# Decoder block on one core: attention scores on all 128 rows, and the gate projections moved beside and behind attention

## Chip, core and metric

The kernel runs on one core of a Trainium2 chip. The metric is device microseconds of one execution; lower is better. Engines are named as the profile names them: PE (TensorE, matmuls), PEld (its weight loads), DVE (VectorE), ACT (ScalarE), POOL (GpSimd), SP (SyncE, which issues most DMAs). L480 is line 480 of the kernel before.

## What is computed

One decoder block for a sequence of 512 tokens and 1024 channels, in float32. Cut to what matters here:

```python
mod = silu(c) @ w_ada + b_ada;  sh1, sc1, g1, sh2, sc2, g2 = split(mod, 6)
proj = (rms_norm(x, pre_norm1) * (1 + sc1) + sh1) @ w_in      # 1024 x 7168
u_glu, q, k, v, gate_logits = proj split into 2048, 1024, 1024, 1024, 2048
u = conv31(ua * sigmoid(ub));  y_conv = silu(layer_norm(u)) @ conv_w_out + conv_b_out
att = softmax(q1 k1^T) v - lam * softmax(q2 k2^T) v           # causal, 8 heads, rope on q and k
y = (g_conv * y_conv + g_att * head_norm(att)) @ w_o          # gates: sigmoid(gate_logits)
x = x + g1 * rms_norm(y, post_norm1)
h = rms_norm(x, pre_norm2) * (1 + sc2) + sh2
x = x + g2 * rms_norm(square(relu(h @ w_ff1)) @ w_ff2, post_norm2)
```

## The kernel before, in words

**Products.** Each float32 operand is split into a high part, rounded to float32r, and a low part, the exact rest; a product is three float32r matmuls, high·high, high·low, low·high (mm3, L205). A projection tile is 128 columns of w_in for all 512 tokens: 8 steps of k with three matmuls of 512 columns (proj, L284). Weights come by SP in loads of 512 KB into three raw buffers; ACT makes the high part, and DVE or ACT with an adding DMA the low part (sub_w, L156).

**Stages on PE.** The start; five pairs of convolution inputs (glu, L537 to L541); 16 gate tiles in a row, evacuated by ACT with a Sigmoid (L543 to L549); four groups of two heads, each with tiles q1, k1, q2, k2 (rope_a, rope_b) and the v tiles (L738 to L749); 8 tiles of the convolution's output (yc, L785); the product with w_o (y, L871 to L883), each of whose four 128-token blocks needs the row gate G1 before its two PSUM banks come free (residual, L819; two such blocks fit into PSUM, L872); then the MLP.

**Attention.** A group's heads are worked in 8 units, each of one head and 128 queries (heads, L611). A unit's scores need, for each of the two softmaxes, three matmuls: L626 multiplies [q high; q low] (128 rows) by [k high; k high]; L627 multiplies q's high 64 rows by k's low 64 rows; L628 adds the causal mask as a bf16 identity times a bf16 mask. ACT does Exp, DVE the maximum, the factors and the difference; PE transposes it (turn) and multiplies by v (weigh). rope_b builds the stacked tiles with four SP DMAs of 128 KB for each q and each k. k's low part stays where DVE wrote it (k_lo). The last DVE steps of a head are norm (L684), scale_out (L693) and turn_back (L702).

**What sets the order of the work beside.** Python generators emit the work beside the projections, and a clock says when. A k-step of a projection ticks 0.65, one of v 0.33 (tick, L252). A tick adds dt times a rate to the background account; each whole unit emits one step of the first generator in the background list, which holds, in this order, conv_steps (124 steps of two DVE multiply-adds), conv_norm (17 steps, L425) and modulations (30 steps, L498). An attention group's generator is resumed when the clock has passed the pause that it named (d1, d2, d3). Program order is the priority with which the compiler's list scheduler fills each engine's queue; on the chip each queue then runs in order. DVE steps of the background are also pinned behind the ninth last DVE operation of the foreground (Beside, L226; lag 8): they can't be placed much ahead of where they were emitted. Before the yc tiles a loop (L753) emits at once what is left of conv_steps and conv_norm. What is left of the modulations is emitted before the eighth yc tile (end_attention, L779).

**Modulations** make s2, sh2 and g1, in that order, by halves of 512 columns: 24 loads of 512 KB (raw_a, L480) into a single buffer, each followed by two DVE operations (L483, L485; under line L235 in the profile), and after four loads a PE transpose and a DVE sum (modc, L492). gate_rows (L510) makes the rows G1 from g1 with eight DVE diagonals, matmuls and ACT copies. The rates before are 0.7 beside u, 0.65 beside the gates, 0.7 beside the first group, 0.5 beside the others, 0.4 beside yc.

Of the kernel before, what the change touches and what calls it, by code (L numbers as in the profile page):

```python
# [17 lines left out]
P = 128  # L18
# [6 lines left out]
CW = 31  # L25
PAD = CW - 1
DFF = 4 * D
EPS = 1e-6
LAM_INIT = 0.2
NEG = -1e30  # L30

CFG = {'raw': 3, 'hi': 3, 'lo': 3, 'ahead': 1, 'araw': 1, 'qk': 10, 'vb': 3, 'plane': 5, 'dma_u': 3, 'dma_g': 1, 'dma_r': 3, 'dma_c': 0, 'dma_o': 0, 'dma_f1': 0, 'dma_f2': 0, 'dma_first': 1, 'r_u': 0.7, 'r_g': 0.65, 'r_p0': 0.7, 'r_p': 0.5, 'r_c': 0.4, 'd1': 2, 'd2': 0.6, 'd3': 0.6, 'evac': 200, 'mod_pe': ((0, 0), (0, 1)), 'wa': 6, 'f_dve': 1, 'wn': 1, 'tail': 2, 'co_att': 7, 'nsplit': 2, 'lag': 8, 'rope_dma': 1, 'ada_dma': 0, 'r_a': 0.15, 'rb': 1, 'tail0': 0, 'sc_dve': 1, 'deep': 1, 'alb': 2, 'h2_act': 0, 'fpre': 2, 'mod_wait': 1, 'pin_mod': 0, 'pin_aT': 0, 'pin_oT': 0, 'ada_rl': 0, 'av_copy': 1, 'nfore': 2, 'kfore': 4, 'wo_at': 5}

# [10 lines left out]
def block_kernel(ctx, tc, io, out):  # L44
# [29 lines left out]

# [1 line left out]
    p0_stack = ExitStack()  # L76
# [28 lines left out]

    ones = const.tile([P, P], F32, name="ones")
    nc.vector.memset(ones, 1.0)
    onesd = const.tile([P, P], F32, name="onesd")
# [4 lines left out]
    nc.vector.memset(epsc, EPS)  # L113
    identb = const.tile([P, P], BF16, name="identb")
    maskb = const.tile([P, P], BF16, name="maskb")

# [11 lines left out]
    def group(slot, name, width=T):  # L128
        w = PAD + T if slot == "U" else T
        pairs = [None] * (KT // 2)  # L130

        def at(ct, sl=slice(0, width)):
            i = ct // 2
            if pairs[i] is None:
                pairs[i] = planes.tile([P, 2, w], F32, tag=f"{slot}{i}", name=f"{name}{i}")
            return pairs[i][:, ct % 2, sl]

        def pair(i):
            at(2 * i)
            return pairs[i]  # L140

        at.pair = pair
        return at
# [10 lines left out]
    nsplit = {}  # L154

    def sub_w(hi, lo, raw, kind):  # L156
        """hi = raw rounded to float32r, lo = the exact rest."""
        nc.scalar.copy(r32(hi), raw)  # L158
        n = nsplit[kind] = nsplit.get(kind, 0) + 1
        every = CFG.get("dma_" + kind, 0)  # L160
        if kind == "first" and n <= CFG["f_dve"]:
            every = 0
        if every == 1 or (every > 1 and n % every):
            nc.scalar.activation(r32(lo), raw, AF.Copy, scale=-1.0)
            nc.gpsimd.dma_start(r32(lo), raw, accum_op=ALU.add)
        else:
            vec.tensor_tensor(r32(lo), raw, hi, ALU.subtract)
# [25 lines left out]

    # weight tiles in the order of their use, split a few tiles ahead of it
    w_specs, w_ready = [], []
# [13 lines left out]

# [39 lines left out]
    clk = dict(t=0.0, bg=0.0, ada=0.0, rate=0.0, resume=0.0)  # L249
# [41 lines left out]
    for ct in range(nfirst, KT):  # L291
        w_specs += [(w_cols, w_in, ct * P, "ua", "u"), (w_cols, w_in, D + ct * P, "ub", "u")]
    for ct in range(KT):
        w_specs += [(w_cols, w_in, 5 * D + ct * P, "gate", "g"), (w_cols, w_in, 6 * D + ct * P, "gate", "g")]
    for g in range(NH // 2):
        for c0 in (2 * D, 3 * D, 2 * D + T, 3 * D + T):
            w_specs.append((w_cols, w_in, c0 + g * P, "qk", "r"))
        w_specs += [(w_v, g, 0), (w_v, g, 1)]
    for ct in range(KT):
        w_specs.append((w_cols, w_co, ct * P, "co", "c"))  # L300

# [1 line left out]
    cwr = p0.tile([CW, D], F32, name="cwr")  # L303
# [25 lines left out]
    for k0, nk in (((0, 1), (1, 1), (2, 2), (4, 2), (6, 2)) if CFG["wn"] == 2 else [(k, 1) for k in range(KT)]):  # L329
# [13 lines left out]
        for j in range(nk):  # L343
# [3 lines left out]
            for i in range(2):  # L347
# [3 lines left out]
                else:  # L351
                    nc.tensor.matmul(po[:, i:i + 1], accs[i][:, js], ones[:, 0:1], start=True, stop=True)
            nc.vector.scalar_tensor_tensor(s1[:, k:k + 1], po[:, 0:1], bada1[:, 8 + k:9 + k], pre1[:, k:k + 1], ALU.add, ALU.mult)
# [21 lines left out]
    make_causal_mask(nc, maskf, NEG)  # L375
    nc.vector.tensor_copy(maskb, maskf)
    nc.vector.tensor_copy(identb, ident)
    pt = ps_t("pb_t")
# [26 lines left out]

# [1 line left out]
    u_done = [False] * KT  # L407
# [102 lines left out]
    def gate_rows(cols, slot):  # L510
        """the columns as rows, the same on every partition"""
        rows = post.tile([P, 2, T], F32, tag=slot, name=f"rows_{slot}")
        for half in range(2):
            dg = plane("diag")
            for i in range(4):
                ct = half * 4 + i
                vec.tensor_scalar(dg[:, i * P:(i + 1) * P], ident, cols[:, ct:ct + 1], None, ALU.mult)
            po = ps_t("rows")
            nc.tensor.matmul(po, ones, dg, start=True, stop=True)
            nc.scalar.copy(rows[:, half], po)  # L520
# [21 lines left out]

    clk["rate"] = CFG["r_g"]  # L543
    for ct in range(KT):
        for dst in (GC, GA):
            o = ps_proj("gate")
            proj(HH, HL, o)
            with tc.high_priority(offset=CFG["evac"]):
                nc.scalar.activation(dst(ct), o, AF.Sigmoid)  # L549

# [1 line left out]
    def rope_a(is_q, name):  # L552
        """projection, and the rotated halves on their way"""
        o = ps_proj(name)
# [10 lines left out]

    def rope_b(part, after):
        is_q, name, f, _ = part
# [4 lines left out]
        A, B = slice(0, HD), slice(HD, P)  # L572
        if is_q:
            hi, lo = plane("qhi"), plane("qlo")
        else:
            hi, lo = plane("khi"), qk("lo")
        with tc.issue_after(after) if CFG["rb"] else ExitStack():
            nc.scalar.copy(r32(hi), f)
        vec.tensor_tensor(r32(lo), f, hi, ALU.subtract)
        t0, t1 = qk("t0"), qk("t1")  # L580
        other = lo if is_q else hi
        nc.sync.dma_start(t0[A], hi[A])
        nc.sync.dma_start(t0[B], other[A])
        nc.sync.dma_start(t1[A], other[B])
        nc.sync.dma_start(t1[B], hi[B])
        return t0, t1, lo

# [23 lines left out]
    def heads(g, q, kk, vts):  # L611
# [3 lines left out]
        def scores(j, qb):  # L615
            rows = slice(j * HD, (j + 1) * HD)
            n = (qb + 1) * P
# [5 lines left out]
            for b in range(2):  # L623
                qt, kt, klo = q[b][j], kk[b][j], kk[b][2]
                o = s[:, b, 0:n]
                nc.tensor.matmul(o, r32(qt[:, qs]), r32(kt[:, 0:n]), start=True, stop=False)  # L626
                nc.tensor.matmul(o, r32(qt[rows, qs]), r32(klo[rows, 0:n]), start=False, stop=False)  # L627
                nc.tensor.matmul(s[:, b, qs], identb, maskb, start=False, stop=True)  # L628
            nm = small("nm", 2)
# [108 lines left out]
    for g in range(NH // 2):  # L738
        clk["rate"] = CFG["r_p"] if g else CFG["r_p0"]
        qk, part = [], None  # L740
        for is_q, name in ((True, "q1"), (False, "k1"), (True, "q2"), (False, "k2")):
            nxt = rope_a(is_q, name)
            if part:
                qk.append(rope_b(part, ins_of(nxt[3])))
            part = nxt
        vts, k2 = v_tiles(g, lambda after: rope_b(part, after))
        q1, k1, q2 = qk
        drain_att()
        att_q.append(heads(g, (q1, q2), (k1, k2), vts))  # L749

# [1 line left out]
    left = 0 if CFG["ada_dma"] else 1  # L752
# [64 lines left out]

# [1 line left out]
    def residual(tb, hv, gr):  # L819
# [64 lines left out]

# [1 line left out]
    F0, F1 = group("HH", "f0"), group("HL", "f1")  # L886
# [113 lines left out]
```

## Time and profile before

| what | value |
|---|---|
| time, median of 3 runs (lowest to highest) | 948.25 us (947.97 to 951.44) |
| span of the profiled execution | 947.9 us |
| busy PE / DVE / ACT / POOL | 884.9 / 585.6 / 420.2 / 118.8 us |
| PE stages: gates / groups / yc / y (stretches read from the trace) | 133 to 220 / 220 to 446 / 446 to 517 / 517 to 578 us |
| mean granted TensorE clock | 0.978 of full speed |

The span is the profiled execution's own time, from the first to the last instruction. A busy share is an average over stages with different limits. Matmuls overlap in the records, so what one costs is read from the distance between two starts.

### The profile page before, as it was taken

How to read it: one execution, taken by the hardware profiler on the slowest of the kernel's cores; microseconds unless marked ns; L12 is line 12 of the kernel's file. 1: busy time of each engine (PE TensorE's matmuls, PEld its weight loads, DVE VectorE, ACT ScalarE, POOL GpSimd, SP SyncE). 2: the span in 40 equal slices, each digit the busy share in tenths (PEclk: the TensorE clock that was granted, in tenths of full speed). 3: DMA queues.
4: the chain of work that ended last, by engine and by line, in shares of the span. 5: the costliest groups of instructions: out<-in, count | busy, mean ns of one | idle time of the engine just before them, and what ended most of it. 6: DMA issues, size and time to landing. Idle time of an engine off the chain costs nothing. (4 is left out here: it accounts for less than half of the span.)

```text
span 947.9 us, 11572 instructions
## 1 busy us (share of the span) xinstructions
PE 884.9 (93%) x4147; PEld 714.6 (75%) x4147; DVE 585.6 (62%) x1084; ACT 420.2 (44%) x770; POOL 118.8 (13%) x162
## 2 busy tenths in 40 slices
PE   6878999999889999798899889999999999999996
PEld 5666888888768777667677668878888788888885
DVE  4857999995679887678699865343222323443522
ACT  4554444544355668644253354433433444223310
POOL 2111011113415142213000011000000000000000
PEclk9999999999989999799899999999999999999999
DMA  9987588988958584875645830464333322232411
GB/s 298 291 212 183 145 178 186 203 189 191 220 111 193 130 175 93 189 191 143 188 155 157 268 88 1 121 179 144 89 89 95 105 89 90 96 105 89 156 44 45
DMA packets 141194, 140.13 MB, mean 148 GB/s; under 512 B 6842, under 2 KB 113459, under 8 KB 141138
## 3 DMA queue, kind: packets, MB, share of 16 engines
q1 hardware_dynamic: 131362, 111.98, 39.7%
q0 software_dynamic: 9696, 27.40, 17.1%
q8 instruction: 32, 0.52, 0.2%
q14 instruction: 24, 0.20, 0.1%
q10 hardware_dynamic: 80, 0.03, 0.0%
HBM read 101.51 MB, written 2.10 MB: 109 GB/s over the span
## 5 line engine op out<-in xcount | busy, mean ns | idle before, releaser
L220 DVE TENSOR_TENSOR lo_ff<-raw_ff,hi_ff 128x1024 fp32r<-128x1024 f32 x56 | 68.5, 1225 | 121.4 <-ACT hi_ff L158 121.4
L158 ACT CAST hi_ff<-raw_ff 128x1024 fp32r<-128x1024 f32 x56 | 58.9, 1052 | 183.0 <-PE ff L207 102.0
L235 DVE SCALAR_TENSOR_TENSOR acc<-u,cw,acc 128x512 f32<-128x512 f32 x200 | 135.3, 738 | 0.0
L206 PE MATMUL ff<-h2h,hi_ff 128*128 128x512 f32 (+2 forms) x272 | 105.3, 388 | 0.0
L207 PE MATMUL ff<-h2l,hi_ff 128*128 128x512 f32 (+2 forms) x272 | 104.3, 384 | 0.0
L208 PE MATMUL ff<-h2h,lo_ff 128*128 128x512 f32 (+2 forms) x272 | 104.2, 384 | 0.0
L208 PE MATMUL f<-hi_ff,fl 128*128 128x512 f32 x192 | 74.7, 389 | 0.0
L207 PE MATMUL f<-lo_ff,fh 128*128 128x512 f32 x192 | 74.7, 389 | 0.0
L206 PE MATMUL f<-hi_ff,fh 128*128 128x512 f32 x192 | 74.7, 389 | 0.0
L563 POOL DMA_DIRECT2D qf<-qs x64 | 52.2, 1284 | 102.1 <-DVE f L220 39.6
L206 PEld LDWEIGHTS ff<-h2h,hi_ff 128*128 128x128 f32 x272 | 51.0, 188 | 11.2 <-issue 0.5
L208 PEld LDWEIGHTS ff<-h2h,lo_ff 128*128 128x128 f32 x272 | 51.2, 188 | 11.0 <-issue 0.2
L207 PEld LDWEIGHTS ff<-h2l,hi_ff 128*128 128x128 f32 x272 | 51.4, 189 | 10.4 <-issue 0.2
L220 DVE TENSOR_TENSOR fl<-f,fh 128x512 fp32r<-128x512 f32 x32 | 22.1, 691 | 59.9 <-PE f L207 55.4
L150 POOL TENSOR_SCALAR ss<-ss 128x1 f32<-128x1 f32 x12 | 3.7, 307 | 403.2 <-ACT junk L824 393.8
L235 DVE SCALAR_TENSOR_TENSOR ada<-raw_a,cs,ada 128x512 f32<-128x512 f32 x56 | 41.9, 748 | 16.2 <-DMA raw_a<-in_w_ada_dram 15.8
L206 PE MATMUL gate<-hh,hi_gate 128*128 128x512 f32 x128 | 49.8, 389 | 0.0
L207 PE MATMUL gate<-hl,hi_gate 128*128 128x512 f32 x128 | 49.8, 389 | 0.0
L208 PE MATMUL gate<-hh,lo_gate 128*128 128x512 f32 x128 | 49.8, 389 | 0.0
L633 ACT ACTIVATE p<-s,nm 128x128 f32<-128x128 f32 (+3 forms) x64 | 33.3, 525 | 29.8 <-DVE nm L220 21.4
L207 PEld LDWEIGHTS f<-lo_ff,fh 128*128 128x128 f32 x192 | 36.0, 188 | 7.6
L206 PEld LDWEIGHTS f<-hi_ff,fh 128*128 128x128 f32 x192 | 36.0, 188 | 7.6
(252 smaller groups left out, 2148.7 us busy)
## 6 DMA issues: line engine op xcount, KB each, us to landing
raw_ff<-in_w_ff_dram SPq DMA_DIRECT2D x56, 512.0 KB
raw_a<-in_w_ada_dram SPq DMA_DIRECT2D x32, 512.0 KB
wa<-in_w_ada_dram SPq DMA_DIRECT2D x16, 512.0 KB
raw_gate<-in_w_in_dram SPq DMA_DIRECT2D x16, 512.0 KB
lo_gate<-raw_gate POOLq DMA_DIRECT2D x16, 512.0 KB, 5.9
raw_qk<-in_w_in_dram SPq DMA_DIRECT2D x16, 512.0 KB
lo_qk<-raw_qk POOLq DMA_DIRECT2D x12, 512.0 KB, 5.8
raw_v<-in_w_in_dram SPq DMA_DIRECT2D x8, 512.0 KB
```

Source lines behind the costliest of these rows:

```text
L150: nc.gpsimd.tensor_scalar(ms[:, 0:1], ms[:, 0:1], ms[:, 1:2] if ms.shape[1] == 2 else 0.0, EPS, ALU.add, ALU.add)
L158: nc.scalar.copy(r32(hi), raw)
L206: nc.tensor.matmul(o, r32(sh), r32(mh), start=first, stop=False)
L207: nc.tensor.matmul(o, r32(sh), r32(ml), start=False, stop=False)
L208: plog[:] = [nc.tensor.matmul(o, r32(sl), r32(mh), start=False, stop=last)]
L220: ins = op(*args, **kw)
L235: return op(*args, **kw)
L563: nc.gpsimd.dma_start(f[b * 32:(b + 1) * 32], sw[s:s + 32], accum_op=ALU.add)
L633: nc.scalar.activation(p[b][:, 0:n], s[:, b, 0:n], AF.Exp, bias=nm[:, b:b + 1], accum_out=lsm[:, b * NTB + qb:b * NTB + qb + 1])
```

## The change

1. Scores: k's low part gets a stacked tile of its own, [k low; k low], so that L627 uses all 128 rows of q's stacked tile. Four more SP DMAs for each k (eight in place of four). The pairs of low tiles live in the buffers of the conv gates (GC), alternating between groups. Low parts of k are first written to the general plane buffers.
2. The mask matmul is float32r times float32r in place of bf16.
3. Gates: the attention gates of heads 2g and 2g+1 are projected right after group g's v tiles; the eight conv gates come after the last group, in the order 4 to 7, 0 to 3, so that a buffer is free when its gate is written.
4. Rates and pauses: 0.45 beside groups and gates; the pauses are 2.6, 1.0, 1.0 in place of 2, 0.6, 0.6.
5. Small: U's rows are padded from 542 to 544 elements; the 128x128 tile of ones becomes one column, and gate_rows uses the tile of 1/1024 with its diagonals scaled by 1024.

```diff
-CFG = {... 'r_g': 0.65, 'r_p0': 0.7, 'r_p': 0.5, ... 'd1': 2, 'd2': 0.6, 'd3': 0.6, ...}
+CFG = {... 'r_g': 0.45, 'r_p': 0.45, ... 'd1': 2.6, 'd2': 1.0, 'd3': 1.0, ...}
-        w = PAD + T if slot == "U" else T
+        w = UW if slot == "U" else T
-    identb = const.tile([P, P], BF16, name="identb")
-    maskb = const.tile([P, P], BF16, name="maskb")
+    identr = const.tile([P, P], F32, name="identr")
+    maskr = const.tile([P, P], F32, name="maskr")
-    for ct in range(KT):
-        w_specs += [(w_cols, w_in, 5 * D + ct * P, "gate", "g"), (w_cols, w_in, 6 * D + ct * P, "gate", "g")]
...
         w_specs += [(w_v, g, 0), (w_v, g, 1)]
+        w_specs += [(w_cols, w_in, 6 * D + ct * P, "gate", "g") for ct in (2 * g, 2 * g + 1)]
+    conv_gates = (4, 5, 6, 7, 0, 1, 2, 3)
+    for ct in conv_gates:
+        w_specs.append((w_cols, w_in, 5 * D + ct * P, "gate", "g"))
...
-                vec.tensor_scalar(dg[:, i * P:(i + 1) * P], ident, cols[:, ct:ct + 1], None, ALU.mult)
+                vec.tensor_scalar(dg[:, i * P:(i + 1) * P], ident, cols[:, ct:ct + 1], float(D), ALU.mult, ALU.mult)
-            nc.tensor.matmul(po, ones, dg, start=True, stop=True)
+            nc.tensor.matmul(po, onesd, dg, start=True, stop=True)
...
-    clk["rate"] = CFG["r_g"]
-    for ct in range(KT):
-        for dst in (GC, GA):
-            o = ps_proj("gate")
-            ...
+    def gate(dst, ct):
+        o = ps_proj("gate")
+        proj(HH, HL, o)
+        with tc.high_priority(offset=CFG["evac"]):
+            nc.scalar.activation(dst(ct), o, AF.Sigmoid)
...
-            hi, lo = plane("qhi"), plane("qlo")
-        else:
-            hi, lo = plane("khi"), qk("lo")
+        hi, lo = plane(f"{name}hi"), plane(f"{name}lo")
...
+        i = 2 * (1 - g % 2) + int(name[1]) - 1
+        kl = planes.tile([P, 2, T], F32, tag=f"GC{i}", name=f"kl{i}")
+        for j, (t, half) in enumerate(((t0, A), (t1, B))):
+            for rows in (A, B):
+                nc.sync.dma_start(t[rows], hi[half])
+                nc.sync.dma_start(kl[rows, j], lo[half])
+        return t0, t1, kl
...
-                nc.tensor.matmul(o, r32(qt[rows, qs]), r32(klo[rows, 0:n]), start=False, stop=False)
-                nc.tensor.matmul(s[:, b, qs], identb, maskb, start=False, stop=True)
+                nc.tensor.matmul(o, r32(qt[:, qs]), r32(kl[:, j, 0:n]), start=False, stop=False)
+                nc.tensor.matmul(s[:, b, qs], r32(identr), r32(maskr), start=False, stop=True)
...
         att_q.append(heads(g, (q1, q2), (k1, k2), vts))
+        for ct in (2 * g, 2 * g + 1):
+            gate(GA, ct)
+    clk["rate"] = CFG["r_g"]
+    for ct in conv_gates:
+        gate(GC, ct)
```

## Rows read from the trace of the kernel before

**Rows 1.** Busy time, share of the span and instructions, by engine (the page).

```profile
PE 884.9 (93%) x4147; PEld 714.6 (75%) x4147; DVE 585.6 (62%) x1084; ACT 420.2 (44%) x770; POOL 118.8 (13%) x162
```

**Rows 2.** Busy time by stretch: gates, groups, yc, y.

```profile
core 0: us, PE busy (x) PEld busy (x) DVE busy (x) ACT busy (x) POOL busy (x), PEclk, DMA share, GB/s
133.00:220.00 87.00, 87.00 (x385) 72.09 (x384) 82.93 (x126) 40.71 (x49) 13.91 (x16) 1.00 0.91 192
220.00:446.00 226.00, 205.10 (x1117) 164.69 (x1115) 172.32 (x356) 130.75 (x303) 67.30 (x80) 0.95 0.71 162
446.00:517.00 71.00, 66.25 (x308) 50.31 (x308) 57.92 (x117) 28.90 (x79) 6.00 (x6) 0.95 0.58 167
517.00:578.00 61.00, 54.07 (x250) 41.15 (x250) 44.02 (x86) 27.91 (x67) 6.58 (x13) 1.00 0.50 153
```

**Rows 3.** PE's waits: engine, line, releaser: us in total, times, longest.

```profile
PE s L626 <- DMA k_t<-khi: 6.1, 1, 6.1
```

**Rows 4.** PE in order of time: y's third block starts (in brackets idle before, releaser).

```profile
550.15 0.50 PE L206 MATMUL y<-woh,yh 128*128 128x512 f32 x1 [1.26 <-DVE t L220]
```

**Rows 5.** DVE in order of time: start, duration; modulations begin, g1 ends.

```profile
382.77 0.68 DVE L235 TENSOR_TENSOR z<-acc,rl 128x512 f32<-128x512 f32 x1
383.37 0.48 DVE L235 TENSOR_SCALAR ada<-raw_a,cs 128x512 f32<-128x512 f32 x1
...
539.95 1.54 DVE L235 SCALAR_TENSOR_TENSOR ada<-raw_a,cs,ada 128x512 f32<-128x512 f32 x2 [0.34 <-DMA raw_a<-in_w_ada_dram]
542.71 0.69 DVE L235 TENSOR_REDUCE g<-modc 128x4 f32<-128x512 f32 x1 [1.22 <-PE modc L492]
...
543.63 0.17 DVE L235 TENSOR_TENSOR g<-g,pbc 128x8 f32<-128x8 f32 x1
```

**Rows 6.** SP in order of time: two raw_a loads that follow each other closely.

```profile
485.44 0.37 SPq L480 DMA_DIRECT2D raw_a<-in_w_ada_dram  x1
...
490.83 0.37 SPq L480 DMA_DIRECT2D raw_a<-in_w_ada_dram  x1
```

**Rows 7.** PE in order of time: a score of 512 columns between two masks, then v.

```profile
302.73 0.23 PE L628 MATMUL s<-maskb,identb 128*128 128x128 bf16 x1
302.77 0.47 PE L626 MATMUL s<-k_t,q_t 128*128 128x512 f32 x1
303.17 0.50 PE L627 MATMUL s<-k_lo,q_t 64*128 64x512 f32 x1
303.60 0.23 PE L628 MATMUL s<-maskb,identb 128*128 128x128 bf16 x1
303.64 0.36 PE L206 MATMUL v<-hi_v,hh 128*128 128x256 f32 x1
303.84 0.28 PE L207 MATMUL v<-lo_v,hh 128*128 128x256 f32 x1
303.96 0.28 PE L208 MATMUL v<-hi_v,hl 128*128 128x256 f32 x1
```

**Rows 8.** PE in order of time: four float32r matmuls of 128 columns.

```profile
315.14 0.56 PE L667 MATMUL av<-vt,al 128*128 128x128 f32 x4
315.53 0.33 PE L208 MATMUL v<-hi_v,hl 128*128 128x256 f32 x1
```

**Rows 9.** ACT in order of time: table loads at the first Exp and around Sqrt.

```profile
261.05 1.28 ACT L633 ACT_TABLE_LOAD   x1
...
356.01 1.28 ACT L450 ACT_TABLE_LOAD   x1
357.30 0.69 ACT L450 ACTIVATE rl<-var,epsc 128x512 f32<-128x512 f32 x1
358.01 1.28 ACT L633 ACT_TABLE_LOAD   x1
359.30 0.58 ACT L633 ACTIVATE p<-s,nm 128x384 f32<-128x384 f32 x1
```

**Rows 10.** The line of k's stacked tiles: DMA issues on SP, min/median/max ns.

```profile
L584 SPq DMA_DIRECT2D k_t<-khi x8: 461/588/597, 245.6 to 458.5; - x8
```

More of the change, by code (lines that the diff above doesn't have):

```diff
@@ L26 @@
 PAD = CW - 1
+UW = 544
 DFF = 4 * D
@@ L30 @@
 NEG = -1e30
-CFG = {'raw': 3, 'hi': 3, 'lo': 3, 'ahead': 1, 'araw': 1, 'qk': 10, 'vb': 3, 'plane': 5, 'dma_u': 3, 'dma_g': 1, 'dma_r': 3, 'dma_c': 0, 'dma_o': 0, 'dma_f1': 0, 'dma_f2': 0, 'dma_first': 1, 'r_u': 0.7, 'r_g': 0.65, 'r_p0': 0.7, 'r_p': 0.5, 'r_c': 0.4, 'd1': 2, 'd2': 0.6, 'd3': 0.6, 'evac': 200, 'mod_pe': ((0, 0), (0, 1)), 'wa': 6, 'f_dve': 1, 'wn': 1, 'tail': 2, 'co_att': 7, 'nsplit': 2, 'lag': 8, 'rope_dma': 1, 'ada_dma': 0, 'r_a': 0.15, 'rb': 1, 'tail0': 0, 'sc_dve': 1, 'deep': 1, 'alb': 2, 'h2_act': 0, 'fpre': 2, 'mod_wait': 1, 'pin_mod': 0, 'pin_aT': 0, 'pin_oT': 0, 'ada_rl': 0, 'av_copy': 1, 'nfore': 2, 'kfore': 4, 'wo_at': 5}
+CFG = {'raw': 3, 'hi': 3, 'lo': 3, 'ahead': 1, 'araw': 1, 'qk': 10, 'vb': 3, 'plane': 5, 'dma_u': 3, 'dma_g': 1, 'dma_r': 3, 'dma_c': 0, 'dma_o': 0, 'dma_f1': 0, 'dma_f2': 0, 'dma_first': 1, 'r_u': 0.7, 'r_g': 0.45, 'r_p': 0.45, 'r_c': 0.4, 'd1': 2.6, 'd2': 1.0, 'd3': 1.0, 'evac': 200, 'mod_pe': ((0, 0), (0, 1)), 'wa': 6, 'f_dve': 1, 'wn': 1, 'tail': 2, 'co_att': 7, 'nsplit': 2, 'lag': 8, 'rope_dma': 1, 'ada_dma': 0, 'r_a': 0.15, 'rb': 1, 'tail0': 0, 'sc_dve': 1, 'deep': 1, 'alb': 2, 'h2_act': 0, 'fpre': 2, 'mod_wait': 1, 'pin_mod': 0, 'pin_aT': 0, 'pin_oT': 0, 'ada_rl': 0, 'av_copy': 1, 'nfore': 2, 'kfore': 4, 'wo_at': 5}
 def r32(ap):
@@ L104, in block_kernel @@
         nc.sync.dma_start(x_sb[:, tb], x_src[tb])
-    ones = const.tile([P, P], F32, name="ones")
-    nc.vector.memset(ones, 1.0)
+    one = const.tile([P, 1], F32, name="one")
+    nc.vector.memset(one, 1.0)
     onesd = const.tile([P, P], F32, name="onesd")
@@ L351, in block_kernel @@
                 else:
-                    nc.tensor.matmul(po[:, i:i + 1], accs[i][:, js], ones[:, 0:1], start=True, stop=True)
+                    nc.tensor.matmul(po[:, i:i + 1], accs[i][:, js], one, start=True, stop=True)
             nc.vector.scalar_tensor_tensor(s1[:, k:k + 1], po[:, 0:1], bada1[:, 8 + k:9 + k], pre1[:, k:k + 1], ALU.add, ALU.mult)
@@ L375, in block_kernel @@
     make_causal_mask(nc, maskf, NEG)
-    nc.vector.tensor_copy(maskb, maskf)
-    nc.vector.tensor_copy(identb, ident)
+    nc.vector.tensor_copy(r32(maskr), maskf)
+    nc.vector.tensor_copy(r32(identr), ident)
     pt = ps_t("pb_t")
@@ L541, in block_kernel @@
         glu(ct, o[:, 0], o[:, 1])
-    clk["rate"] = CFG["r_g"]
-    for ct in range(KT):
-        for dst in (GC, GA):
-            o = ps_proj("gate")
-            proj(HH, HL, o)
-            with tc.high_priority(offset=CFG["evac"]):
-                nc.scalar.activation(dst(ct), o, AF.Sigmoid)
+    def gate(dst, ct):
[3 more added lines that the diff above has]
+            nc.scalar.activation(dst(ct), o, AF.Sigmoid)
     def rope_a(is_q, name):
@@ L564, in rope_a, with rope_b @@
         return is_q, name, f, evac
-    def rope_b(part, after):
+    def rope_b(g, part, after):
         is_q, name, f, _ = part
@@ L572, in rope_b @@
         A, B = slice(0, HD), slice(HD, P)
-        if is_q:
-            hi, lo = plane("qhi"), plane("qlo")
-        else:
-            hi, lo = plane("khi"), qk("lo")
+        hi, lo = plane(f"{name}hi"), plane(f"{name}lo")
         with tc.issue_after(after) if CFG["rb"] else ExitStack():
@@ L580, in rope_b @@
         t0, t1 = qk("t0"), qk("t1")
[L581 to L586, printed above, removed]
+        if is_q:
+            for t, half in ((t0, A), (t1, B)):
+                nc.sync.dma_start(t[A], hi[half])
+                nc.sync.dma_start(t[B], lo[half])
+            return t0, t1
+        i = 2 * (1 - g % 2) + int(name[1]) - 1
[5 more added lines that the diff above has]
+        return t0, t1, kl
     def v_tiles(g, between):
@@ L615, in scores @@
         def scores(j, qb):
-            rows = slice(j * HD, (j + 1) * HD)
             n = (qb + 1) * P
@@ L623, in scores @@
             for b in range(2):
-                qt, kt, klo = q[b][j], kk[b][j], kk[b][2]
+                qt, kt, kl = q[b][j], kk[b][j], kk[b][2]
                 o = s[:, b, 0:n]
                 nc.tensor.matmul(o, r32(qt[:, qs]), r32(kt[:, 0:n]), start=True, stop=False)
-                nc.tensor.matmul(o, r32(qt[rows, qs]), r32(klo[rows, 0:n]), start=False, stop=False)
-                nc.tensor.matmul(s[:, b, qs], identb, maskb, start=False, stop=True)
+                nc.tensor.matmul(o, r32(qt[:, qs]), r32(kl[:, j, 0:n]), start=False, stop=False)
+                nc.tensor.matmul(s[:, b, qs], r32(identr), r32(maskr), start=False, stop=True)
             nm = small("nm", 2)
@@ L738, in block_kernel @@
     for g in range(NH // 2):
-        clk["rate"] = CFG["r_p"] if g else CFG["r_p0"]
+        clk["rate"] = CFG["r_p"]
         qk, part = [], None
@@ L743, in block_kernel @@
             if part:
-                qk.append(rope_b(part, ins_of(nxt[3])))
+                qk.append(rope_b(g, part, ins_of(nxt[3])))
             part = nxt
-        vts, k2 = v_tiles(g, lambda after: rope_b(part, after))
+        vts, k2 = v_tiles(g, lambda after: rope_b(g, part, after))
         q1, k1, q2 = qk
```

## The prediction

> **What bounds the kernel now.** I read the page's busy times first: PE is busy for 93% of the span [rows 1], so one would look for PE work to save. The stretches [rows 2] then say where there is air: none beside the gates (87.0 of 87 us), 20.9 us beside the groups (226 less 205.1), 4.8 beside yc, 6.9 beside y. PE's waits name small ones, such as 6.1 us once for k's stacked tile [rows 3]. In PE's order of time one of 1.26 us looks harmless and is the one to follow: the third block of y waits until 550.15 for the DVE tile t, which needs the row gate G1 [rows 4]; PE was ready at 548.9. DVE's order of time [rows 5] shows the modulations begin at 383.37, right behind a z step, the last part of the convolution's norm, and end with g1 at 543.8. The modulations are one chain: 24 loads into a single buffer, each waiting for the two DVE operations of the one before. Its 23 steps from the first load's DVE work to the last's take 539.95 − 383.37 = 156.6 us, 6.8 each. From 543.8 it takes gate_rows and t some 6 us to 550.15, so PE and this chain arrive together. Two things therefore bound the stretch up to there: PE, and the convolution followed by the modulations. A gain on PE alone is worth about 1.3 us.
>
> **PE's saving.** From one mask to the next a score of 512 columns takes 303.60 − 302.73 = 0.87 us [rows 7]: 0.04 from the bf16 mask to L626, 0.40 to L627, 0.43 to the next mask. A 512-column matmul of a gate tile takes 87.0/384 = 0.227 [rows 2], so the 64-row matmul costs about 0.17 before it and 0.20 behind it. After the change all three have 128 rows: 2 × 0.227, and a mask of 128 columns in float32r, which I take from the four av matmuls of that shape, (315.53 − 315.14)/4 = 0.10 [rows 8]. That is 0.55, a saving of 0.32. With fewer columns the same two switches go, but a 128-column matmul costs 0.10 and not a quarter of 0.227; I take 0.27 as the mean. 64 such scores give 17.3 us, 4.3 a group. Bounds: nothing, if the delay is not from the 64 rows, and 20.5 us, if all save 0.32.
>
> **Where PE is when attention ends.** From 133.0 on PE has the same tiles in another order: 16 gate tiles, 87.0 us; 16 q and k tiles of the same form, 87.0; 384 v matmuls at 0.12 [rows 7], 46.1. In the 226 us of the groups PE was busy for 205.1; less 87.0 and 46.1 that leaves 72.0 for three groups' attention, 24.0 each. After the change that is 19.7, and all four groups lie before yc: 78.8. Without idle time yc begins at 133.0 + 87.0 + 87.0 + 46.1 + 78.8 = 431.9. Idle time was 20.9 for three groups, 7.0 each; four give 28: 460. DVE doesn't set this: it was busy for 255 of the 313 us before 446 [rows 2], and what it gains (the fourth group's attention) and loses (the modulations) are about equal.
>
> **When each background step comes.** This is arithmetic on the code. The clock runs 52.0 beside the five u pairs (80 k-steps of 0.65), 83.2 beside 16 gates, 31.36 a group. Before: 52 × 0.7 + 83.2 × 0.65 + 31.36 × 0.7 + 94.1 × 0.5 = 159.5 steps up to yc. The convolution and its norm need 124 + 17 = 141, so they end 18.5/0.5 = 37 units before yc, inside the third group; the trace agrees, z at 382.77 [rows 5]. After: 52 × 0.7 + 208.6 × 0.45 = 130.3. The last 10.7 steps of the norm are then emitted in a lump at yc, and no step of the modulations comes before yc. Beside yc 36.4 × 0.4 = 14.6 of their 30 steps are emitted, the rest at once before the last tile. So the chain that ends together with PE today starts later.
>
> **How much later.** Its first DVE operation is pinned behind the ninth last foreground DVE operation. Counting back at the first yc tile: two low parts of yc's weights, turn_back, four of scale_out, two of norm: it can't come before the last head's norm. With the new pauses the last weigh is emitted at 248.3 on the clock and yc starts at 260.6, 19 k-steps later, 19 × 3 × 0.227 = 12.9 us. So the chain starts at about 460 − 12.9 + 1.5 (the norm's own few short operations) = 448.6, against 383.4. Then 23 steps. Before they took 6.8 each, among attention's DVE work; the closest pair of loads was 490.83 − 485.44 = 5.4 apart [rows 6]. Beside yc there will be no attention, but w_o's and yc's weights share SP: I take 5.8, nearer the dense pair, 133.4 us. From the last load's DVE work to g1 it was 543.8 − 539.95 = 3.85. So g1 ends at 448.6 + 133.4 + 3.9 = 586, 42 us later than 543.8. What follows g1 is unchanged in work (404 us to the end); PE will stand ready for it, worth the 1.3 us wait and a little more: −2.
>
> **Edits that I cost at nothing, and their cover.** The lump of the norm: from the mean on it is 15 DVE operations of some 0.68 us (the z row of [rows 5]), the Sqrt with its table load, 2.0 [rows 9], four reciprocals and the first z, some 18 us that PE waits at yc. yc (192 matmuls, 44 us) and two blocks of y (96, 22 us) fit with them between 460 and 586, with 42 us to spare; if the chain came early, these 18 us would stand in the sum. k's four more DMAs: 32 × 0.59 [rows 10] = 19 us of SP's time, behind which weights and raw_a queue, over 300 us; for the first scores of a group, 2.4 us more wait each, 9.4 in all if nothing covers it. k's low part now takes a plane buffer until its DMAs have landed; planes are asked for by DVE and ACT, which have air. U's 544 elements, the one column and the scaled diagonals change no count of instructions.
>
> **Table loads.** The first Exp after the gates brought a table load of 1.28 us (261.05), and Sqrt between Exps brought two [rows 9]. With Sigmoids between Exps some 14 of the 16 gates will bring two: 28 × 1.28 = 36 us of ACT. ACT idled 46 us beside the gates and 95 beside the groups [rows 2], so I let this be hidden; all of it on the path is the upper bound. In the rows nothing but the load lies between the neighbours: Sqrt ends at 357.99, the load starts at 358.01, Exp at 359.30. The Trainium skill (ScalarE: Activation LUTs, What ACT_TABLE_LOAD costs) gives about 1283 ns for the load, as measured here, and some 1380 ns of drain besides, 2.66 us a switch. These rows show no such drain; by the page's figure ACT would lose an estimated 74 us.
>
> **The sum.** 947.9 + 42 − 2 = 988 for a profiled execution; its span is 0.35 below the median of 948.25, so 988 stands. Bounds of the forecast: no idle time and steps of 5.4 give a start at 420.5 and g1 at 548.5, 952; twice the idle time and steps of 6.8 give 476 and 636, 1040.
>
> **Rivals.** *Faster: the chain isn't late.* If the scheduler places the modulations in DVE's gaps during the groups, PE's saving and an yc without attention count. PE would finish y's second block at 460 + 18 + 44 + 22 = 544, against 548.9; with the lump spread out as well, at 526. That gives 925 to 943, say 932. It decides at a start before about 543.8 − 3.9 − 124 = 416. Against it: the pin, and DVE's order today, norm first and modulations right behind [rows 5]. For it: the pin is my count from the code, which no row shows. *Same:* start near 420 and steps of 5.4: 948 to 952. *Slower by ACT:* the table loads delay each Exp, attention ends up to 36 us later, the chain with it: 1000 to 1024. For it: each Exp stands between a unit's scores and its transposes; against it: ACT's 141 us of idle time. The Trainium skill (ScalarE: Activation LUTs, Table sets: the hidden batching unit) has the rule that speaks against the change here: calls should be batched by table set. *The 128 rows save nothing:* the penalty in [rows 7] has another cause; the chain starts 17 us later: 1005.
>
> **Chances.** Forecast 0.69, faster 0.12, same 0.07, ACT 0.08, no saving 0.04. A measurement of this kernel can tell about 0.5%, 4.7 us, from no change. Faster 0.12, same 0.07, slower 0.81. The range from 943 to 1018 leaves out the faster rival and the upper ends.
>
> **What would show it.** Right: ada's first DVE operation after 420 and behind the last norm; g1's last operation at 560 to 610; PE idle by some 50 us between 455 and 590, released by ada or t; mask to mask at most 0.6 us; a table load beside most gates. Wrong: ada before 416, or loads less than 5 us apart; then the time falls below 948. L627 still 0.4 us from its mask would refute the saving.

## The result, and the profile after

The kernel after takes **1030.2 us** (median of 4 runs, 1027.88 to 1036.02) against 948.11 us (947.23 to 951.44) for the kernel before on the same chip: a ratio of 1.087, 95% interval 1.083 to 1.091. It is 82 us slower; the forecast was 40 us slower, with 1018 as the upper end. Lines of the kernel after are one to three higher than before up to the heads' code (L629 to L631 are the score matmuls, L236 the background's DVE steps).

The page's busy line of the kernel after, to be laid beside [rows 1]:

```profile
PE 876.6 (85%) x4147; PEld 725.6 (71%) x4147; DVE 589.5 (57%) x1084; ACT 446.6 (43%) x791; POOL 117.6 (11%) x162
```

PE is busy for 8 us less and DVE for 4 us more, so the 82 us are waiting. Busy time by stretch (columns as in [rows 2]) says where:

```profile
core 0: us, PE busy (x) PEld busy (x) DVE busy (x) ACT busy (x) POOL busy (x), PEclk, DMA share, GB/s
133.00:413.00 280.00, 251.47 (x1407) 220.15 (x1406) 218.79 (x442) 166.96 (x361) 81.18 (x96) 0.95 0.80 174
413.00:459.00 46.00, 43.50 (x215) 35.13 (x213) 32.19 (x67) 34.30 (x63) 6.38 (x7) 1.00 0.60 138
459.00:476.00 17.00, 2.38 (x3) 0.79 (x3) 12.95 (x20) 8.32 (x12) 0.00 (x0) 0.52 0.11 31
476.00:525.00 49.00, 47.45 (x199) 38.00 (x199) 40.55 (x55) 23.19 (x30) 0.00 (x0) 0.96 0.69 226
525.00:622.00 97.00, 30.26 (x115) 22.99 (x113) 39.46 (x64) 6.11 (x9) 0.00 (x0) 0.64 0.41 124
622.00:1028.00 406.00, 389.62 (x1728) 317.81 (x1728) 148.53 (x207) 145.77 (x239) 10.34 (x24) 0.98 0.29 90
```

Two stretches stand out. From 459 to 476 PE does almost nothing: that is the lump of the convolution's norm. From 525 to 622 it is busy for 30 of 97 us. PE's waits (engine, line, releaser: us in total, times, longest) name both:

```profile
PE modc L495 <- DVE ada L236: 61.8, 7, 20.5
...
PE var L451 <- DVE sqs L236: 8.4, 1, 8.4
PE yc L207 <- ACT ch L463: 8.3, 1, 8.3
```

The lump is 8.4 + 8.3 = 16.7 us. The large one is at the transposes modc of the modulations, which wait for ada; at t in front of y's third block [rows 4] PE waits only 1.8 us. The forecast had named both, ada or t. PE in order of time (in brackets the idle time before, and its releaser):

```profile
554.46 1.09 PE L495 MATMUL modc<-ident,ada 128*128 128x128 f32 x4 [11.44 <-DVE ada L236]
...
575.99 1.09 PE L495 MATMUL modc<-ident,ada 128*128 128x128 f32 x4 [20.44 <-DVE ada L236]
...
597.56 1.09 PE L495 MATMUL modc<-ident,ada 128*128 128x128 f32 x4 [20.48 <-DVE ada L236]
...
619.37 0.63 PE L495 MATMUL modc<-ident,ada 128*128 128x128 f32 x4 [3.89 <-DVE ada L236]
```

Each group of four loads ends in the transposes of one sum, and from one such group to the next are 21.5 us. Between them PE has little else that it could do, because DVE's queue is held by the chain too. Of the 96 matmuls of y's first two blocks 60 are done by 543, and the other 36 start at 604.53: they need the last of the four merges, which make y's input yh. DVE and PE in order of time:

```profile
528.02 0.74 DVE L221 SCALAR_TENSOR_TENSOR gc<-yc,pbc,gc 128x512 f32<-128x512 f32 x1
...
601.48 0.48 DVE L236 TENSOR_SCALAR ada<-raw_a,cs 128x512 f32<-128x512 f32 x1 [1.91 <-DMA raw_a<-in_w_ada_dram]
601.88 0.68 DVE L221 TENSOR_TENSOR y<-gc,ga 128x512 f32<-128x512 f32 x1
```

```profile
604.53 0.79 PE L207 MATMUL y<-woh,yh 128*128 128x512 f32 x1 [5.89 <-ACT yh L784]
```

The merge's last input, gc, was made at 528.8, but the code emits it behind what is left of the modulations, and DVE came to it 73 us later. This cost nothing on top here: the two blocks were done by 615.5, and the rows G1, which wait for the chain's end, start at 622.18 (last section). What the chain itself does is in DVE's order of time, to be laid beside [rows 5]:

```profile
479.34 0.69 DVE L236 TENSOR_TENSOR z<-acc,rl 128x512 f32<-128x512 f32 x1
479.94 0.48 DVE L236 TENSOR_SCALAR ada<-raw_a,cs 128x512 f32<-128x512 f32 x1
...
617.68 1.54 DVE L236 SCALAR_TENSOR_TENSOR ada<-raw_a,cs,ada 128x512 f32<-128x512 f32 x2 [3.92 <-DMA raw_a<-in_w_ada_dram]
...
620.95 0.17 DVE L236 TENSOR_TENSOR g<-g,pbc 128x8 f32<-128x8 f32 x1
```

The chain begins 479.94 − 383.37 = 96.6 us later than before. Its 23 steps take 137.7 us in place of 156.6 (5.99 each in place of 6.8), and the rest to g1 takes 0.4 less, so g1 ends at 621.1 instead of 543.8, 77.3 us later. From there to the end it takes 407.3 us against 404.1. 77.3 + 3.2 = 80.5 us, the whole difference of the two spans (1028.4 − 947.9).

PE's saving is there all the same. PE in order of time, two scores of 512 columns, beside [rows 7]:

```profile
264.12 0.22 PE L631 MATMUL s<-maskr,identr 128*128 128x128 f32 x1
264.18 0.44 PE L629 MATMUL s<-k_t,q_t 128*128 128x512 f32 x1
264.46 0.39 PE L630 MATMUL s<-kl,q_t 128*128 128x512 f32 x1
264.69 0.22 PE L631 MATMUL s<-maskr,identr 128*128 128x128 f32 x1
```

From mask to mask it is 0.57 us, against 0.87 before. Over all 64 scores, whose widths differ, the mean distance falls from 0.708 to 0.417 us, worked out from all the starts: 0.29 × 64 = 18.6 us.

### The profile page after: what moved, and what is told of

Read it like the earlier page. It is cut to its first block, busy times and chain, and to the rows that moved or that the text cites. A ratio compares the mean times of both kernels' runs of the same rounds, so it can differ in the third digit from the quotient of the medians.

```text
span 1028.4 us, 11672 instructions
## 1 busy us (share of the span) xinstructions
PE 876.6 (85%) x4147; PEld 725.6 (71%) x4147; DVE 589.5 (57%) x1084; ACT 446.6 (43%) x791; POOL 117.6 (11%) x162
## 4 chain that ended last, share of the span: by engine, by line
issue 38%; DMA 19%; PE 16%; DVE 16%; ACT 7%; POOL 2%; SPq 1%; DVEq 0%; POOLq 0%; ACTq 0%
DMA raw_a<-in_w_ada_dram 7%; DVE acc L236 5%; DVE ada L236 3%; DMA qf<-qs 2%; DMA wa<-in_w_ada_dram 2%; PE gate L209 2%; PE gate L207 2%; PE gate L208 2%; DMA raw_wo<-in_w_o_dram 1%; DMA kl<-k1lo 1%; DMA q_t<-q1lo 1%; DMA lamv<-in_lambda_k_dram 1%; ACT L636 1%; ACT p L636 1%; PE uab L209 1%
## 5 line engine op out<-in xcount | busy, mean ns | idle before, releaser
L236 DVE SCALAR_TENSOR_TENSOR acc<-u,cw,acc 128x512 f32<-128x512 f32 x200 | 141.3, 742 | 0.0
L236 DVE SCALAR_TENSOR_TENSOR ada<-raw_a,cs,ada 128x512 f32<-128x512 f32 x56 | 42.0, 750 | 61.3 <-DMA raw_a<-in_w_ada_dram 60.2
L495 PE MATMUL modc<-ident,ada 128*128 128x128 f32 x32 | 6.4, 336 | 61.8 <-DVE ada L236 61.8
L207 PE MATMUL gate<-hh,hi_gate 128*128 128x512 f32 x128 | 54.4, 425 | 2.6 <-DVE vt L221 2.6
L495 PEld LDWEIGHTS modc<-ident,ada 128*128 128x128 f32 x32 | 4.3, 169 | 64.7 <-issue 60.8
```

What stands on the lines that cost most here:

```text
L207: nc.tensor.matmul(o, r32(sh), r32(mh), start=first, stop=False)
L236: return op(*args, **kw)
L495: nc.tensor.transpose(po[:, i * P:(i + 1) * P], acc[:, i * P:(i + 1) * P], ident)
```

## The experiments

Four theories were put to the test. **Late chain:** the modulations' single-buffered chain, started late, makes the whole loss. **Lump:** the norm in front of yc makes a good part of it. **DVE:** DVE's work ahead of yc sets the pace, so PE's saving can't be cashed. **ACT:** the table loads do. Ratios are to the kernel before.

**The modulations on an account of their own**, so that they are emitted early at a low rate (e1_mods_own_account):

```diff
-    (ada_q if CFG["ada_dma"] else bg_q).append(modulations())
+    ada_q.append(modulations())
-    left = 0 if CFG["ada_dma"] else 1
-    while len(bg_q) > left:
+    while bg_q:
```

> The changed kernel, with the modulations taken out of the list behind the convolution and emitted from their own account (0.15 a tick, which the kernel has already), so that they end beside the third and fourth groups. Theory (the late chain of 24 loads makes all of the loss): g1 ends before 450, PE's waits for modc go, the lump of the norm (17 us) stays: yc begins at 476 to 485, the whole 940 to 958. Rival (attention, table loads or PE's own order make the loss): still above 1000.

999.5 us, ratio 1.053 [1.048, 1.058], in neither range. The chain now begins at 73 us, and yc only at 514.4, 38.7 later than in the kernel after: it comes that much later with 48 DVE operations and 24 loads moved ahead of it. Whether the operations, the loads or the buffers do it was not separated. The MLP lost time as well: the background clock had run on with an empty list, the steps of g2 were then emitted in a burst, and PE waited 13.8 us for modc. This is an effect of the edit, so it was repeated with that clock set to zero before the steps of g2 are listed, `clk["bg"] = 0.0` (e11_own_account_reset):

> The run with the modulations in their own account, with the same reset. Theory: PE's 13.8 us of waits for modc in the MLP go: 980 to 988; yc still begins at 510 to 518, some 38 us later than in the changed kernel, since the modulations' DVE work stands before yc. Rival: 993 to 1002.

983.9 us, 1.036 [1.031, 1.040]; yc at 512.8. Without that effect the early chain still leaves 36 us of the loss, as much as yc begins later (37).

**The kernel before with a late chain** (e2_before_mods_late): the modulations are listed only when yc begins.

```diff
-    (ada_q if CFG["ada_dma"] else bg_q).append(modulations())
...
     clk["rate"] = CFG["r_c"]
+    bg_q.append(modulations())
```

> The kernel before, with nothing changed but that the modulations are emitted only from the first yc tile on. Theory: the chain starts at 446 to 452 in place of 383, takes 23 steps of 6.0 to 6.6, g1 ends at 588 to 605, the whole 995 to 1012. Rival (the chain is not what bounds): 948 to 955.

979.9 us, 1.034 [1.029, 1.038], less than expected. The first ada came at 427.5 and yc at 432.4, 14 us earlier than before, with the modulations gone from beside attention. Still the same kind of wait appeared in a kernel without any other part of the change, PE behind DVE's sum at modc:

```profile
PE modc L492 <- DVE ada L235: 18.0, 4, 11.0
```

A chain 44 us later costs 32 us there.

**The rates of before in the kernel after** (e3_rates_of_before): 0.65, 0.7 and 0.5 in place of 0.45.

> The changed kernel with the background rates of the kernel before (0.7 beside the first group, 0.5 beside the others, 0.65 beside the conv gates). By the emission arithmetic 155 steps are emitted before yc, so the norm ends some 22 clock units, about 24 us, before yc. Theory: no lump (17 us less on PE) and a chain that starts at about 435 to 450: g1 at 576 to 592, the whole 983 to 1000. Rival (DVE is full beside attention, so that steps emitted earlier do not run earlier): 1020 to 1035.

1008.4 us, 1.062 [1.058, 1.067], in neither range. The lump is gone, but yc begins at 482.0, 6.3 later than with it: PE now waits 12.6 us for ACT's hi_gate instead, and the lump's 16.7 us were not to be had back by these rates. Here ACT is the limit: it is busy for 29.75 of the 30 us from 430 to 460, and 11.5 of them are nine table loads, since the Sqrt and Silu of the norm fall between the gates' Sigmoids and attention's Exps. The chain again starts right behind the norm, ada at 446.55 after the last z at 445.94.

**The old scores in the kernel after** (e4_old_scores_in_after): L630 multiplies 64 rows, and the mask is bf16.

```diff
-                nc.tensor.matmul(o, r32(qt[:, qs]), r32(kl[:, j, 0:n]), ...)
-                nc.tensor.matmul(s[:, b, qs], r32(identr), r32(maskr), ...)
+                nc.tensor.matmul(o, r32(qt[rows, qs]), r32(kl[rows, j, 0:n]), ...)
+                nc.tensor.matmul(s[:, b, qs], identb, maskb, ...)
```

> The changed kernel with L627's low product on 64 rows again and the bf16 mask again; the stacked low tiles and their DMAs stay. Theory (a switch of rows costs 0.27 us a score, 17 us before yc, and the chain starts that much later): 1042 to 1052, mask to mask 0.85 us at 512 columns. Rival (the 128 rows save nothing): 1026 to 1034.

1042.9 us, 1.100 [1.096, 1.104], some 12 us more than the kernel after. PE in order of time, one score between two masks:

```profile
272.43 0.23 PE L632 MATMUL s<-maskb,identb 128*128 128x128 bf16 x1
272.47 0.48 PE L630 MATMUL s<-k_t,q_t 128*128 128x512 f32 x1
272.88 0.50 PE L631 MATMUL s<-kl,q_t 64*128 64x512 f32 x1
273.31 0.23 PE L632 MATMUL s<-maskb,identb 128*128 128x128 bf16 x1
```

The 0.88 us of before is back. The first two parts of the change are a gain, and about two thirds of it reach the end. The run puts the 64 rows and the bf16 mask back together, so it doesn't show which share of the delay belongs to which.

**Two buffers for raw_a** (e5_two_raw_a_buffers): 'araw' 2, and 'qk' 8 in place of 10 to make room for it.

> The changed kernel with two buffers for the modulations' loads in place of one; to make room the stacked tiles get 8 buffers in place of 10, one group's worth. Theory (the chain's steps are load, two operations, load, one after the other): steps fall from 6.0 to 3.5 to 4.5 us, the chain still starts behind the norm at about 480, g1 at 564 to 588, the whole 970 to 996. Rival (the steps are set by the queue of SP or by the DMA engines): steps stay above 5.5, 1022 to 1034.

976.6 us, 1.029 [1.024, 1.034]: 54 us of the loss gone by a faster chain, with its start (479.84) and yc's (475.59) as in the kernel after. DVE in order of time, the chain's first and last operations:

```profile
479.84 0.48 DVE L236 TENSOR_SCALAR ada<-raw_a,cs 128x512 f32<-128x512 f32 x1
...
566.14 1.54 DVE L236 SCALAR_TENSOR_TENSOR ada<-raw_a,cs,ada 128x512 f32<-128x512 f32 x2 [1.93 <-DMA raw_a<-in_w_ada_dram]
```

86.3 us for the 23 steps, 3.75 each in place of 5.99; PE's waits for modc fall from 61.8 to 17.8 us.

**No modulation loads at all** (e6_no_modulation_loads): s2, sh2 and g1 come from their biases, which leaves out 24 loads, 48 DVE operations and their transposes.

> The changed kernel without the products of the modulations: s2, sh2 and g1 are made from their biases alone, so that 24 loads, their 48 DVE operations and 24 transposes are left out. This takes the chain away and moves it nowhere. Theory: yc still begins at about 476, y's third block at 476 + 44 + 22 + 2 = 544, the whole 940 to 952, so that the late chain accounts for 78 to 90 us. Rival (something else behind yc is late too, such as w_o's weights or the merge): above 965.

970.0 us, 1.020 [1.015, 1.025], which the rival allowed for and the theory didn't, but with the burst of g2's steps as in e1 (PE waited 14.8 us for modc in the MLP). Repeated with the clock set to zero (e10_no_loads_reset):

> The run without the modulations' products again, with the background account set to zero before the last modulation (g2) is put into the list. There the list had been empty, the account had run on, and all of g2's steps were emitted at once early in the first MLP product, where PE then waited 14.8 us for its transposes. Theory: those waits go, nothing else moves: 950 to 957, so that the late chain accounts for 73 to 80 of the 82 us. Rival: no change, 963 to 972.

948.5 us, 0.999 [0.996, 1.002], a little below the range. The longest waits of PE in this run:

```profile
PE aT L653 <- DVE p L221: 12.5, 3, 6.7
PE var L451 <- DVE sqs L236: 8.4, 1, 8.4
PE yc L207 <- ACT ch L463: 8.3, 1, 8.3
```

modc is gone from the top, the lump is still there, and the time is that of the kernel before. Without the late chain nothing of the 82 us is left; the lump (16.7) then about cancels the scores' saving (18.6). The two kernels emit the same work up to yc, yet yc begins at 481.8 in e6's profiled execution and at 475.7 in e10's. So where two runs' starts of yc, read from one execution each, differ by some 6 us or less, the difference is not shown.

**A buffer of its own for the chain's sum** (e9_own_sum_buffers). The running sum ada sits in one of the five plane buffers, which the norm uses too. ('qk' is 8 here as well, which left yc's start unchanged in e5.)

```diff
-  acc = plane("ada") if base == 5 or not CFG["ada_rl"] else ap_.tile([P, T], F32, tag="rl", name="ada")
+  acc = plane("ada") if base == 5 else ap_.tile([P, T], F32, tag="own", name="ada", bufs=2)
```

> The changed kernel with two buffers of their own for the modulations' running sums, which otherwise take one of the five plane buffers that the convolution's norm also uses (8 buffers for the stacked tiles make the room, as in the run with two load buffers, where yc began unchanged). It asks why the chain began at 480, behind the norm's last step, and not at the last head's norm at about 445. If the plane buffers held it: ada begins at 443 to 460, g1 at 585 to 603, the whole 993 to 1012. If the order of emission held it (the norm's operations go first on DVE): ada begins at 475 to 481, 1024 to 1034.

1012.2 us, 1.067 [1.061, 1.072]. DVE in order of time:

```profile
437.96 0.15 DVE L221 TENSOR_TENSOR l<-l 128x4 f32<-128x4 f32 x1
438.03 0.48 DVE L236 TENSOR_SCALAR ada<-raw_a,cs 128x512 f32<-128x512 f32 x1
...
443.29 0.68 DVE L236 TENSOR_TENSOR tot<-acc 128x512 f32<-128x512 f32 x1
```

The chain begins at 438.0, earlier than expected and ahead of the norm's first operation (tot), 42 us earlier than in the kernel after. What held it until the last z was a plane buffer. The gain is only 18 us: beside the norm the 23 steps take 591.37 − 438.03 = 153.3 us, 6.67 each in place of 5.99, yc begins at 484.9, and PE still waits 48.4 us for modc.

**The attention gates ahead of the groups**, as in the order of before, with the rates and pauses of before (e7_attention_gates_first):

> The changed kernel with the attention gates projected before the groups, as before; scores, mask, conv gates behind the groups as in the change; rates and pauses of the kernel before. 153 steps are emitted before yc, the norm ends some 17 clock units into the conv gates. Theory (the chain bounds): yc begins at 445 to 465 without a lump, the chain starts at 415 to 430, g1 at 555 to 575, the whole 960 to 980. Rival (what loses the time is the gates beside attention, not the chain): 930 to 948.

1006.7 us, 1.059 [1.055, 1.063], a miss. yc begins at 473.6 where 445 to 465 was expected, the chain at 444.5 where 415 to 430 was.

**The same with two raw_a buffers** (e8_gates_first_two_buffers):

> The kernel of the run before with two buffers for the modulations' loads and 8 for the stacked tiles. Theory: the chain, started at 415 to 430, takes 85 to 100 us and ends before PE has finished y's second block at 445 to 465 + 66, so that PE bounds: the whole 918 to 940, faster than both kernels. Rival (DVE is as full as PE up to here, so that PE's saving is not kept): 945 to 960.

948.9 us, 1.000 [0.997, 1.003], in the rival's range. The chain is no longer late, and the version ties with the kernel before, though each score costs 0.29 us less. PE's waits between 133 and 580 us that DVE ends, the longest of this version:

```profile
PE aT L651 <- DVE al L221: 10.1, 4, 4.6
PE av L667 <- DVE on L221: 5.1, 3, 3.4
PE modc L495 <- DVE ada L236: 4.7, 5, 2.8
PE q L207 <- DVE vt L221: 4.5, 1, 4.5
PE aT L651 <- DVE p L221: 4.0, 4, 1.8
PE mean L437 <- DVE al L221: 3.8, 1, 3.8
```

and of the kernel before:

```profile
PE av L664 <- DVE on L220: 5.1, 4, 2.9
PE modc L492 <- DVE ada L235: 4.3, 2, 3.4
PE x2T L851 <- DVE xn L220: 3.2, 3, 1.2
PE av L664 <- DVE f L220: 2.3, 1, 2.3
```

All of PE's waits in this stretch add up to 50.0 us here and 32.1 before; those for DVE to 42.0 and 21.3. The 18 us that PE saves (busy for 866.6 us in place of 884.9) come back as 18 us of waiting, mostly for the DVE steps inside attention units: the waits of aT, av and oT for DVE add up to 22.2 us here and 9.7 before.

**Without the gates' Sigmoid** (e12_gates_without_sigmoid): a plain copy in its place, which leaves out the sigmoid of the gates and so the table loads around it.

> The changed kernel with Copy in place of the gates' Sigmoid, so that no table is switched for a gate; the gates are left without their sigmoid. Theory (28 loads of 1.28 us are hidden by ACT's idle time): yc begins at 472 to 478, the whole 1024 to 1034. Rival (each load delays an Exp, and attention with it): yc begins 10 to 36 us earlier, the whole 992 to 1020.

1025.6 us, 1.080 [1.075, 1.084], against 1.087 [1.083, 1.091]: 5 to 7 us, with intervals that touch. ACT had 6 table loads in place of 31, 25 × 1.28 = 32 us less. So the table loads don't make the loss of the kernel after; in e3, where the norm runs between the conv gates, they do hold PE up.

**Can the tie of e8 be turned into a gain?** First, low parts of all q, k and v weights (v's are counted with them) by ACT and an adding DMA, in e8 (e13_gates_first_low_by_dma, 'dma_r' 1 in place of 3) and as a control in the kernel before (e14_before_low_by_dma):

> The version with the attention gates first and two raw_a buffers (948.9 us), with the low part of every q and k weight made by ACT and an adding DMA in place of two in three: about 8 subtractions of some 1.2 us leave DVE. Theory: up to yc DVE is as full as PE there, so DVE's length sets when yc begins and PE's saving is lost in it; with some 10 us less DVE work before yc, yc begins at 463 to 468 in place of 472.9 and the kernel takes 938 to 944, faster than both. Rival: DVE is not the limit, yc begins at 471 to 475 as without the edit, and it takes 946 to 953.

> The same edit in the kernel before, as the control. Theory: there PE and the chain of the modulations arrive together and DVE is not the limit, so it takes 945 to 952, no change that can be told. Rival: 8 subtractions less on DVE let the convolution's norm and the chain behind it start up to 10 us earlier and it gains as much, 938 to 944.

960.7 us, 1.012 [1.010, 1.015], and 965.2 us, 1.017 [1.013, 1.020]: both slower, in none of the ranges. DVE's work from 133 to 445 us fell from 252.95 to 241.18 us in e13, yet yc began at 478.4 in place of 472.9. PE got a new wait that e8 has not, and the control has it too (5.4 us, once):

```profile
PE v L208 <- DMA lo_v<-raw_v: 7.2, 2, 4.0
```

So less DVE work did not bring yc forward; but the edit made DMA waits of its own, so it doesn't clear DVE either. Then more time for the attention units, by the pauses of after (e15_gates_first_long_pauses) and by rates of 0.55 and 0.6 in place of 0.65 and 0.7 (e16_gates_first_lower_rates):

> The version with the attention gates first and two raw_a buffers (948.9 us), with the pauses of the kernel after (2.6, 1.0, 1.0 in place of 2, 0.6, 0.6). In that version PE waits some 28 us beside groups and conv gates for DVE's al, p and on, the steps of the attention units. Theory: these waits, not DVE's sum of work, eat PE's saving, and longer pauses give DVE the time: at least 8 us of them go, yc begins at 462 to 468, and it takes 936 to 944, faster than both kernels. Rival: the waits move behind the last group, where fewer projections are left as cover; yc begins at 471 to 480 and it takes 946 to 958.

> The same version with the rates 0.55 beside the gates and 0.6 beside the first group in place of 0.65 and 0.7: about 16 x 5.2/2 x 0.1 = 4 to 5 steps of the convolution come later. Theory that DVE's order eats the saving: the attention units wait less for DVE, yc begins 3 to 8 us earlier, the chain begins some 5 to 9 us later (450 to 454) but with two buffers still ends ahead of need: 940 to 947. Rival: what is taken out of the groups comes back as a lump ahead of yc or as a later chain: 948 to 960.

972.5 us, 1.026 [1.020, 1.031], and 964.5 us, 1.015 [1.010, 1.021]. Both went the way of the rival, and past its range. With longer pauses the waits moved behind the last group (the last transposes aT start at 491.0 in place of 463.8) and yc began at 493.7; with lower rates yc began at 477.9 and the chain at 465.6. No version beat the kernel before; where DVE's waits in e8 could be saved stays open.

## Why the prediction was wrong in size

**Right: what bounds.** PE and the modulations arrived together, the change put the chain late, and a gain on PE showed only as far as it brought the chain's start forward (12 of the 18.6 us, e4). e10, without the chain, is back at the time of before.

**Right: PE's saving.** 17.3 us forecast, 18.6 measured; e4 brings the delay back. That it comes from the 64 rows and not in part from the bf16 mask was not shown.

**Right by its sum, in part by luck: where PE is when attention ends.** 460 was forecast for yc without the lump; it was 475.7 − 16.7 = 459.0. From 133 to 459 PE was busy for 295.0 us, where the sum has 298.9, and idle for 31.0, where it has 28. The lump was forecast at 18 us and measured at 16.7. But the idle time was carried over from a stretch with the modulations in it: e2, which takes them out of the order of before, has 13.1 us of it up to yc in place of 20.9, and the kernel after, without them too, has 31.0. So "DVE doesn't set this" isn't shown, and in another order yc came later (e1 with the chain ahead of it; e3, where PE waited for ACT). That PE's wait at the lump is covered by the late chain was right; but the norm itself stood ahead of the chain, as follows.

**Wrong: how much later.** This is the step that failed: "it can't come before the last head's norm", hence a start at 448.6. It was a lower bound from one condition, taken as the start. The chain started at 479.94, 31.3 us later, and e9 shows the second condition: its sum needs a plane buffer, and the norm, lumped at yc, held the planes until its last z. The rows hinted at it: before, ada starts 0.60 us after the start of a z [rows 5], after it does so again (479.34, 479.94), and in e3 (445.94, 446.55). I read that neighbourhood as the order of the code and let it go when the norm moved by a lump. The bound was mis-timed as well: in e9 the first ada comes at 438.03, right behind l<-l at 437.96, the first of the two DVE operations of the last head's norm. My count back by nine ends at that operation, but it needs only the sums l and runs about 10 us ahead of the second, which comes at 447.80.

**A term too small: the steps.** 5.8 us forecast, 5.99 measured, 4.3 us over 23 steps. The dense pair of [rows 6] was no pessimistic choice: at 612.22 and 617.68 DVE's operations are 5.46 apart even with little else going on, and beside yc they are further apart.

**A term of the wrong sign: behind g1.** −2 us forecast, +3.2 measured. PE stood ready as forecast, with two blocks of y done, but it had been mostly idle and ran on the lower clock at first (last section): from the first matmul of the rows G1 to y's third block it took 628.78 − 622.18 = 6.6 us, against 550.15 − 544.85 = 5.3 before, 1.3 us of the 3.2, and from the first to the tenth matmul of that block 632.79 − 628.78 = 4.0 us, against 552.33 − 550.15 = 2.2 before, another 1.8. With 31.3 + 4.3 − 0.4 + 5.2 = 40.4 us the terms give the distance from the forecast of 988 to the span of 1028.4.

**Costs at nothing.** k's four more DMAs: PE's wait for k's stacked tile is 6.0 us once, as before [rows 3], though no run took them away alone and in e1 PE waited 9.5 us for the new tile kl. The table loads were mostly hidden: there were 21 more of them than before, against 28 forecast, and they cost 5 to 7 us by e12. ACT's table loads of the kernel after at the two lines with most of them, Exp and the gates' Sigmoid (busy time, mean ns of one | idle before):

```profile
L636 ACT ACT_TABLE_LOAD x13 | 16.7, 1283 | 5.4 <-DVE nm L221 5.3
L550 ACT ACT_TABLE_LOAD x13 | 16.7, 1283 | 0.2
```

The 13 loads at the Sigmoid have 0.2 us of idle time before them in all, and the one that starts at 257.21 and takes 1.28 us is followed by its Sigmoid at 258.51. The Trainium skill (ScalarE: Activation LUTs, What ACT_TABLE_LOAD costs) names a drain of some 1380 ns beside each load; these rows show none. Its rule that calls should be batched by table set (Table sets: the hidden batching unit) was worth no more than the 5 to 7 us of e12 in the kernel after.

**The range** was too narrow on top: the prediction's own bounds reached 1040, and the end was set at 1018, which left the upper ends out. The start was the larger unknown.

## What to carry to other kernels

When a chain of loads and sums is moved, list everything that its first step needs (its place in the queue, its input, and its output buffer) and take the last of them; a neighbour that ends just before it in the trace of before may be the holder of a buffer. A background chain that is emitted ahead of other work holds that work in every queue that it uses: here PE waited at each of its outputs, and DVE came to a ready merge 73 us late. And a saving on the busiest engine may come back as waits for the second: here 18 us of matmul time against 18 us more of waits, mostly for DVE, with the chain repaired.

## What the runs showed of the hardware

PE's clock fell in its long waits and cost more behind them. PE by stretches of 10 us right behind g1, in the kernel after:

```profile
622.00:632.00 10.00, 7.33 (x12) 3.55 (x13) 4.25 (x11) 3.30 (x8) 1.73 (x4) 0.50 0.02 7
632.00:642.00 10.00, 10.00 (x46) 8.21 (x45) 5.75 (x13) 5.05 (x15) 0.86 (x2) 0.91 0.00 0
```

PE had been busy for 30 of the 97 us before; the granted clock is 0.50, the lower level of 1.2 GHz, in the first stretch, and near the upper one in the next. It had been at 1.00 from 610 to 615, in the last of y's matmuls for the first two blocks; from 615.5 to 622.18 PE ran only the four transposes of modc. The two matmuls that make the rows G1 (each recorded as two) take twice their time of before. PE in order of time, the first of them, after and before:

```profile
622.18 2.04 PE L522 MATMUL rows<-diag,onesd 128*128 128x512 f32 x2 [2.18 <-DVE diag L221]
```

```profile
544.85 1.10 PE L519 MATMUL rows<-diag,ones 128*128 128x512 f32 x2
```

A second buffer brought the chain of 512 KB loads from 5.99 to 3.75 us a step, while DVE's two operations of a step take 1.54 us. With one buffer a load starts only when the sum before it is done, and its landing lies open in every step. In the kernel after, one sum ends at 541.90 + 1.54 = 543.44; the next load from its issue, and DVE's next step:

```profile
543.46 3.81 DMA raw_a<-in_w_ada_dram
547.36 1.54 DVE L236 SCALAR_TENSOR_TENSOR ada<-raw_a,cs,ada 128x512 f32<-128x512 f32 x2 [3.93 <-DMA raw_a<-in_w_ada_dram]
```
